# Sum over 1024 columns: 16-row bulk loads, two access patterns and stores instead of three, and the last store ahead of the closing waits

## Chip, cores and metric

One core of a Trainium2 chip. The metric is the time of one execution in device microseconds; medians of several runs. The experiments ran on three different chips, so kernels are compared through the kernel before, which ran in each.

## The reference

```python
batch, seq, dim = 32, 512, 1024          # x is float32, 67.1 MB
def reference(x, divisor):               # divisor = 1024.0
    return (np.sum(x, axis=-1) / divisor).astype(np.float32)
```

16384 rows of 1024 numbers: 128 rows for each of 128 partitions.

## The kernel before

SyncE (SP) issues all loads and stores. Bulk tiles rotate through three buffers; VectorE (DVE) reduces a tile in one instruction, ScalarE (ACT) takes some rows near the end, GpSimd (POOL) scales the result. The last rows come in ever smaller loads, down to two half rows `pa` and `pb`. The rows of a partition lie in two parts of `x`: its first 16 rows (64 KB from one partition to the next, called the pitch) and its other 112 (448 KB). A load or store "lands" when its semaphore, a counter that others wait on, tells that it is complete.

```python
F, L = 16, 16
M = J - F - L                     # J = 128 rows per partition
W = M + L
x_first = bass.AP(tensor=x.tensor, offset=0, ap=[[F * D, P], [D, F], [1, D]])
x_main = bass.AP(tensor=x.tensor, offset=P * F * D, ap=[[W * D, P], [D, M], [1, D]])
x_last = bass.AP(tensor=x.tensor, offset=P * F * D + M * D, ap=[[W * D, P], [D, L], [1, D]])
first = [(2, 0), (14, 0)]                         # (rows, of which on ACT)
main = [(14, 0)] * 5 + [(14, 4), (12, 5)]
last = [(9, 4), (4, 2), (2, 1)]
# ... cut
for loads, src, dst in ((first, x_first, res0), (main, x_main, res)):
    j = 0
    for rows, on_act in loads:
        t = bulk.tile([P, 14, D], F32, name="t")
        load(t[:, :rows, :], src[:, j : j + rows, :])
        d = rows - on_act
        for i in range(d, rows):
            act_sum(dst[:, j + i : j + i + 1], t[:, i, :])
        nc.vector.reduce_sum(out=dst[:, j : j + d], in_=t[:, :d, :], axis=AX)
        j += rows
    nc.gpsimd.tensor_scalar_mul(out=dst, in0=dst, scalar1=scale)
# ... cut: the last loads; stores of res0 and res
dve_mean(pb[:, D - c : D - c + 1], pa, by=1.0)
dve_mean(fin[:, j:], pb)
tc.keep_in_program_order(nc.sync.dma_start(out=o_last, in_=fin))
```

`close_while_storing` rearranges the program's end: SyncE waits for everything but the last store (`drain`), issues that store, takes part in the closing barriers of all five engines, and at last waits until the store has landed. In a closing barrier every engine reports that it is there (SyncE's report is a DRAIN instruction) and goes on when all have reported.

```python
end.instructions = [
    with_sync(drain, on_wait=tuple(needs.values())),
    with_sync(store, on_wait=(done,), on_update=(add,)),   # done: VectorE's last instruction
    *end.instructions[1:-1],                               # the two closing barriers
    with_sync(last, on_update=(sub,)),                     # the store has landed
]
```

Of the kernel before, what the change touches and what calls it, by code (L numbers as in the profile page):

```python
# [9 lines left out]
F32 = mybir.dt.float32  # L10
ADD = mybir.AluOpType.add
COPY = mybir.ActivationFunctionType.Copy
AX = mybir.AxisListType.X
# [23 lines left out]
def with_sync(i, on_wait=None, on_update=None):  # L37
    s = i.sync_info
    return copy.replace(
        i,  # L40
        sync_info=mybir.SyncInfo(
            on_wait=s.on_wait if on_wait is None else on_wait,
            on_update=s.on_update if on_update is None else on_update,
        ),
    )
# [21 lines left out]
def close_while_storing(nc, landed):  # L67


    body, end = nc.main_func.blocks[1], nc.main_func.blocks[-1]  # L70
    store = [i for i in body.instructions if i.engine == SP and type(i).__name__ == "InstDMACopy"][-1]
    (lane,) = store.sync_info.on_update
    drain = end.instructions[0]
    assert drain.engine == SP and type(drain).__name__ == "InstDrain"
    needs = {w.id: w for w in drain.sync_info.on_wait}
    assert needs[lane.id].wait_value > lane.update_value
    needs[lane.id] = dataclasses.replace(
        needs[lane.id], wait_value=needs[lane.id].wait_value - lane.update_value
    )

    (done,) = [w for w in store.sync_info.on_wait if w.ant_name.startswith("DVE_")]
    assert needs[done.id].wait_value == done.wait_value
    del needs[done.id]
    own = dict(sync_type="semaphore", id=landed.num, ant_name=landed.name)
    add = mybir.SyncUpdate(update_mode="sem-add-imm", update_value=16, **own)
    sub = mybir.SyncUpdate(update_mode="sem-sub-imm", update_value=16, **own)
    last = nc.sync.wait_ge(landed, 16).ins
    assert nc.main_func.blocks[-1].instructions[-1].name == last.name
    body.instructions = [i for i in body.instructions if i.name != store.name]
    end.instructions = [  # L90
        with_sync(drain, on_wait=tuple(needs.values())),
        with_sync(store, on_wait=(done,), on_update=(add,)),
        *end.instructions[1:-1],
        with_sync(last, on_update=(sub,)),
    ]


@with_exitstack
def kernel(
    ctx: ExitStack,  # L100
    tc: tile.TileContext,
    x: bass.AP,
    divisor: float,
    out: bass.AP,
):
    nc = tc.nc
    landed = nc.alloc_semaphore("landed")
    nc.at_finalize(start_loads_at_once)
    nc.at_finalize(latest_wait_first)
    nc.at_finalize(lambda nc: close_while_storing(nc, landed))  # L110
    xf = x.flatten_outer_dims()
    N, D = xf.shape
    P = nc.NUM_PARTITIONS
    scale = 1.0 / float(divisor)
    J = N // P
    assert J * P == N


    F, L = 16, 16
    M = J - F - L  # L120
    W = M + L
    x_first = bass.AP(tensor=x.tensor, offset=0, ap=[[F * D, P], [D, F], [1, D]])
    x_main = bass.AP(tensor=x.tensor, offset=P * F * D, ap=[[W * D, P], [D, M], [1, D]])
    x_last = bass.AP(tensor=x.tensor, offset=P * F * D + M * D, ap=[[W * D, P], [D, L], [1, D]])
    o_first = bass.AP(tensor=out.tensor, offset=0, ap=[[F, P], [1, F]])
    o_main = bass.AP(tensor=out.tensor, offset=P * F, ap=[[W, P], [1, M]])
    o_last = bass.AP(tensor=out.tensor, offset=P * F + M, ap=[[W, P], [1, L]])


    first = [(2, 0), (14, 0)]  # L130
    main = [(14, 0)] * 5 + [(14, 4), (12, 5)]
    last = [(9, 4), (4, 2), (2, 1)]
    assert sum(n for n, _ in first) == F
    assert sum(n for n, _ in main) == M and sum(n for n, _ in last) == L - 1

    pad = ctx.enter_context(tc.tile_pool(name="pad", bufs=1))
    pad.tile([P, 224], F32, name="pad")
    bulk = ctx.enter_context(tc.tile_pool(name="bulk", bufs=3))
    one = ctx.enter_context(tc.tile_pool(name="one", bufs=1))
    psum = ctx.enter_context(tc.tile_pool(name="junk", bufs=4, space=bass.MemoryType.PSUM))  # L140


    c = 512
    t4 = one.tile([P, 4, D], F32, name="t4")
    t2 = one.tile([P, 2, D], F32, name="t2")
    pa = one.tile([P, 768], F32, name="pa")[:, :c]
    pb = one.tile([P, D - c + 16], F32, name="pb")[:, : D - c + 2]
    res0 = one.tile([P, F], F32, name="res0")
    res = one.tile([P, M], F32, name="res")
    fin = one.tile([P, L], F32, name="fin")  # L150
    nc.gpsimd.memset(pb[:, D - c :], 0.0)  # L151

    def load(dst, src):
        tc.keep_in_program_order(nc.sync.dma_start(out=dst, in_=src))  # L154

    def act_sum(dst, src, by=1.0):
        junk = psum.tile([P, D], F32, name="junk")
        nc.scalar.activation(junk, src, COPY, scale=by, accum_out=dst)  # L158

    def dve_mean(dst, src, by=scale):  # L160


        h = src.shape[-1] // 2
        nc.vector.tensor_tensor_reduce(  # L164
            out=src[:, :h], in0=src[:, :h], in1=src[:, h:], scale=by, scalar=0.0,
            op0=ADD, op1=ADD, accum_out=dst,
        )

    for loads, src, dst in ((first, x_first, res0), (main, x_main, res)):
        j = 0  # L170
        for rows, on_act in loads:
            t = bulk.tile([P, 14, D], F32, name="t")
            load(t[:, :rows, :], src[:, j : j + rows, :])
            d = rows - on_act
            for i in range(d, rows):
                act_sum(dst[:, j + i : j + i + 1], t[:, i, :])
            nc.vector.reduce_sum(out=dst[:, j : j + d], in_=t[:, :d, :], axis=AX)  # L177
            j += rows
        nc.gpsimd.tensor_scalar_mul(out=dst, in0=dst, scalar1=scale)  # L179
    j = 0  # L180
    for rows, on_act in last:
        t = bulk.tile([P, 14, D], F32, name="t")[:, :rows, :] if rows > 4 else t4 if rows == 4 else t2
        load(t, x_last[:, j : j + rows, :])
        d = rows - on_act
        for i in range(rows):
            if i < d:
                dve_mean(fin[:, j + i : j + i + 1], t[:, i, :])
            else:
                act_sum(fin[:, j + i : j + i + 1], t[:, i, :], by=scale)
        j += rows  # L190
    load(pa, x_last[:, j, :c])
    load(pb[:, : D - c], x_last[:, j, c:])


    tc.keep_in_program_order(nc.sync.dma_start(out=o_first, in_=res0))
    tc.keep_in_program_order(nc.sync.dma_start(out=o_main, in_=res))

    dve_mean(pb[:, D - c : D - c + 1], pa, by=1.0)
    dve_mean(fin[:, j:], pb)
    tc.keep_in_program_order(nc.sync.dma_start(out=o_last, in_=fin))  # L200
# [35 lines left out]
```

## Time and profile before

| | before |
|---|---|
| time, median of the 6 runs beside the changed kernel | 160.75 us (160.63 to 160.82) |
| span of the profiled run | 159.1 us, its time 160.59 us |
| VectorE, ScalarE busy | 117.2 us, 18.5 us |
| DMA queue | 98.2% of 16 engines' span |

The span goes from the first to the last recorded instruction; the time is longer by 1.5 to 1.6 us. The lines of the profile that carry the argument are in the prediction.

### The profile page before, as it was taken

What the parts mean: (1) busy time and instruction counts of PE and PEld (TensorE: products, weight loads), DVE (VectorE), ACT (ScalarE), POOL (GpSimd) and SP (SyncE); (2) the same over time, 40 slices, a digit from 0 to 9 for tenths busy, and PEclk for the clock granted to TensorE, in tenths of its full rate; (3) what the DMA queues carried; (4) which work ended last, traced back from release to release, by engine and by line L of the source; (5) the groups of instructions that cost most, each with busy time, mean ns of one, the idle gap of its engine ahead of it and who ended that gap; (6) DMA issues with size and microseconds to landing.
All of it is one profiled execution on the core that took longest, in us unless ns stands there. A gap on an engine that the chain in (4) does not pass through costs nothing.

```text
span 159.1 us, 147 instructions
## 1 busy us (share of the span) xinstructions
DVE 117.2 (74%) x29; ACT 18.5 (12%) x33; POOL 1.0 (1%) x7
## 2 busy tenths in 40 slices
DVE  0500059995999599977999599959995996395643
ACT  3000000000000000000000000000000900390684
POOL 0000000000000000000000000000000000001000
DMA  8999999979999999789999999699999999999894
GB/s 303 422 461 461 461 461 461 433 317 404 461 461 461 461 461 461 317 375 461 461 461 461 461 461 418 303 433 461 461 461 429 396 396 445 445 445 445 375 406 159
DMA packets 2448, 67.18 MB, mean 422 GB/s; under 512 B 656, under 2 KB 656, under 8 KB 912
## 3 DMA queue, kind: packets, MB, share of 16 engines
q1 hardware_dynamic: 2448, 67.18, 98.2%
HBM read 67.11 MB, written 0.07 MB: 422 GB/s over the span
## 4 chain that ended last, share of the span: by engine, by line
DMA 77%; DVE 21%; SPq 1%; issue 0%; DVEq 0%
DMA t<-in_x_dram 56%; DMA pb<-in_x_dram 21%; DVE res L177 20%; SPq L154 1%; DVE pb L164 0%; DVEq L231 0%
## 5 line engine op out<-in xcount | busy, mean ns | idle before, releaser
L177 DVE TENSOR_REDUCE res<-t 128x14 f32<-128x14336 f32 (+3 forms) x9 | 111.2, 12360 | 34.1 <-DMA t<-in_x_dram 34.1
L158 ACT ACTIVATE junk<-t 128x1024 f32<-128x1024 f32 x16 | 16.2, 1013 | 136.9 <-DMA t<-in_x_dram 136.9
L164 DVE CUSTOM_DVE_ANT_0 t<-t 128x512 f32<-128x512 f32 x8 | 5.1, 690 | 6.1 <-DMA t<-in_x_dram 6.1
L158 ACT ACTIVATION_READ_ACCUMULATOR junk<-t 128x1 f32 x16 | 3.0, 187 | 0.0
L179 POOL TENSOR_SCALAR res<-res 128x16 f32<-128x16 f32 (+1 forms) x2 | 0.7, 352 | 143.3 <-DVE res L177 143.3
L158 ACT ACT_TABLE_LOAD x1 | 1.3, 1283 | 1.7 <-PEq L217 1.7
L164 DVE DVE_READ_ACCUMULATOR2_ANT fin<- 128x1 f32 x9 | 0.8, 83 | 0.0
L164 DVE CUSTOM_DVE_ANT_0 pb<-pb 128x257 f32<-128x257 f32 x1 | 0.4, 428 | 0.2 <-DMA pb<-in_x_dram 0.2
L164 DVE CUSTOM_DVE_ANT_0 pa<-pa 128x256 f32<-128x256 f32 x1 | 0.4, 426 | 0.0
L151 POOL MEMSET pb<- 128x2 f32 x1 | 0.1, 99 | 1.3 <-POOLq L217 1.3
L217 POOL MEMSET const-bfloat16-1.0<- 128x1 bf16 x1 | 0.1, 102 | 0.0
L217 POOL MEMSET const-uint8-127<- 128x1 uint8 x1 | 0.1, 101 | 0.0
L217 POOL MEMSET const-float32-0.0<- 128x1 f32 x1 | 0.1, 98 | 0.2 <-issue 0.2
L217 POOL MEMSET const-float32-1.0<- 128x1 f32 x1 | 0.1, 98 | 0.0
L164 DVE DVE_READ_ACCUMULATOR2_ANT pb<- 128x1 f32 x1 | 0.1, 84 | 0.0
## 6 DMA issues: line engine op xcount, KB each, us to landing
t<-in_x_dram SPq DMA_DIRECT2D x7, 7168.0 KB, 35.6
t<-in_x_dram SPq DMA_DIRECT2D x1, 6144.0 KB, 33.3
t<-in_x_dram SPq DMA_DIRECT2D x1, 4608.0 KB, 27.2
t<-in_x_dram SPq DMA_DIRECT2D x2, 1024.0 KB, 19.2
t<-in_x_dram SPq DMA_DIRECT2D x1, 2048.0 KB, 31.7
pa<-in_x_dram SPq DMA_DIRECT2D x1, 256.0 KB, 33.9
pb<-in_x_dram SPq DMA_DIRECT2D x1, 256.0 KB, 33.9
out_dram<-res SPq DMA_DIRECT2D x1, 48.0 KB, 11.6
```

The source lines that it names most:

```text
L151: nc.gpsimd.memset(pb[:, D - c :], 0.0)
L154: tc.keep_in_program_order(nc.sync.dma_start(out=dst, in_=src))
L158: nc.scalar.activation(junk, src, COPY, scale=by, accum_out=dst)
L164: nc.vector.tensor_tensor_reduce(out=src[:, :h], in0=src[:, :h], in1=src[:, h:], scale=by, scalar=0.0, op0=ADD, op1=ADD, accum_out=dst,)
L177: nc.vector.reduce_sum(out=dst[:, j : j + d], in_=t[:, :d, :], axis=AX)
L179: nc.gpsimd.tensor_scalar_mul(out=dst, in0=dst, scalar1=scale)
L217: nc = _bacc.Bacc("TRN2", target_bir_lowering=False, num_devices=1)
```

## The change

Its intent: fewer and larger loads, one store fewer, and a last store that need not queue behind the closing waits. Core of the diff (the tile shapes follow; a tile for 4 rows goes, `pa` shrinks):

```diff
     end.instructions = [
+        with_sync(store, on_wait=store.sync_info.on_wait, on_update=(add,)),
         with_sync(drain, on_wait=tuple(needs.values())),
-        with_sync(store, on_wait=(done,), on_update=(add,)),
         *end.instructions[1:-1],
@@
-    F, L = 16, 16
-    M = J - F - L
-    W = M + L
-    x_first = ...  x_main = ...  x_last = ...  o_first = ...  (cut)
-    first = [(2, 0), (14, 0)]
-    main = [(14, 0)] * 5 + [(14, 4), (12, 5)]
+    L = 16
+    M = J - L
+    x_main = bass.AP(tensor=x.tensor, offset=0, ap=[[M * D, P], [D, M], [1, D]])
+    x_last = bass.AP(tensor=x.tensor, offset=P * M * D, ap=[[L * D, P], [D, L], [1, D]])
+    main = [(2, 0), (14, 0)] + [(16, 0)] * 4 + [(16, 4), (16, 7)]
@@
-            t = bulk.tile([P, 14, D], F32, name="t")
+        t = bulk.tile([P, 16, D], F32, name="t")
@@
-    tc.keep_in_program_order(nc.sync.dma_start(out=o_first, in_=res0))
     tc.keep_in_program_order(nc.sync.dma_start(out=o_main, in_=res))
```

## The prediction

> **What bounds the kernel now.** I read the page from the top: busy shares, the transfer rows, the chain that ended last, then the timeline of VectorE (DVE) and of the end. VectorE is busy 117.2 of 159.1 us, ScalarE (ACT) 18.5 us, so neither fills the span. The DMA queue does:
>
> ```profile
> DMA packets 2448, 67.18 MB, mean 422 GB/s; under 512 B 656, under 2 KB 656, under 8 KB 912
> q1 hardware_dynamic: 2448, 67.18, 98.2%
> ```
>
> 98.2% of the 16 DMA engines' time is in packets, and 67.11 of the 67.18 MB are the input, read once. The chain that ended last seems to say something else, 77% DMA and 20% of VectorE's reduce. That share is how the view follows a load back to the wait of its issue, a buffer freed by a reduce. It doesn't mean that the queue stood still, which the spacing of the reduces shows:
>
> ```profile
> 21.60 15.09 DVE L177 TENSOR_REDUCE res<-t 128x14 f32<-128x14336 f32 x1 [14.60 <-DMA t<-in_x_dram]
> ...
> 38.51 15.09 DVE L177 TENSOR_REDUCE res<-t 128x14 f32<-128x14336 f32 x1 [1.83 <-DMA t<-in_x_dram]
> 55.46 15.09 DVE L177 TENSOR_REDUCE res<-t 128x14 f32<-128x14336 f32 x1 [1.86 <-DMA t<-in_x_dram]
> 72.39 15.09 DVE L177 TENSOR_REDUCE res<-t 128x14 f32<-128x14336 f32 x1 [1.84 <-DMA t<-in_x_dram]
> 89.28 15.09 DVE L177 TENSOR_REDUCE res<-t 128x14 f32<-128x14336 f32 x1 [1.80 <-DMA t<-in_x_dram]
> 106.19 15.09 DVE L177 TENSOR_REDUCE res<-t 128x14 f32<-128x14336 f32 x1 [1.83 <-DMA t<-in_x_dram]
> ```
>
> Each reduce starts when its load lands, each after about 1.8 us of idling, and the landings are (106.19 - 21.60) / 5 = 16.92 us apart. In the trace's packet records a 14-row load is 8 packets of 57344 bytes per DMA engine at 2.116 us (median), and 8 x 2.116 = 16.93 us. So there is no gap between one load and the next: the engines run packet after packet. The rate row has dips (317 GB/s beside 461), but the load that landed across one (38.51 to 55.46, 16.95 us) took no longer than the one without (55.46 to 72.39, 16.93 us); I take the dips for the booking of packets and not for pauses.
>
> The end is a series of its own:
>
> ```profile
> 122.67 0.47 SPq L154 DMA_DIRECT2D pa<-in_x_dram  x1
> ...
> 123.19 0.44 SPq L154 DMA_DIRECT2D pb<-in_x_dram  x1
> 123.68 0.44 SPq L195 DMA_DIRECT2D out_dram<-res  x1
> ...
> 145.89 0.34 SPq L196 DMA_DIRECT2D out_dram<-res  x1
> ...
> 157.15 0.43 DVE L164 CUSTOM_DVE_ANT_0 pb<-pb 128x257 f32<-128x257 f32 x1 [0.16 <-DMA pb<-in_x_dram]
> 157.50 0.08 DVE L164 DVE_READ_ACCUMULATOR2_ANT fin<- 128x1 f32 x1
> 157.62 0.33 SPq L200 DMA_DIRECT2D out_dram<-fin  x1
> ```
>
> ```profile
> pb<-in_x_dram SPq DMA_DIRECT2D x1, 256.0 KB, 33.9
> out_dram<-res SPq DMA_DIRECT2D x1, 48.0 KB, 11.6
> out_dram<-res SPq DMA_DIRECT2D x1, 8.0 KB, 33.6
> out_dram<-fin SPq DMA_DIRECT2D x1, 8.0 KB, 1.4
> ```
>
> The last column is us from issue to landing. The last half row pb lands at 123.19 + 33.9 = 157.1; VectorE ends at 157.50 + 0.08 = 157.58; the last store is issued at 157.62 and lands 1.4 us later, at 159.02; the span ends at 159.05. So the span is about 4.7 us to the first landing (start, and 2 rows), 152.4 us of packets, and 1.9 us of end. The timed run is 160.74 us, 1.6 us above the span.
>
> **What the Trainium skill says.** "DMA: Bandwidth & Descriptors", section "Where 436 GB/s comes from", gives 435.2 GB/s as the ceiling of a core's DMA. The trace agrees: from the 8192-byte packet (0.309 us) to the 57344-byte one (2.116 us) the slope is 36.76 ns per 1000 bytes, or 27.2 GB/s per engine and 435 GB/s for 16. What is left over is 0.309 - 0.301 = 0.008 us per packet. The same page, "Queues, rings and completion order", has each engine consume descriptors in ring order. The trace agrees: the 8 KB store was issued at 123.68, 34 us ahead of the end, and landed at 157.3, behind pb. The same page, "Latency and other measured facts" (row "HBM row pitch at large powers of two"), tells of copies slowed by pitches from 512 KiB up; it lists neither 64 nor 448 KB. Here the first 16 rows have 64 KB between partitions and the rest 448 KB: the 14-row load of the first part took 21.60 - 4.72 = 16.88 us, the 448 KB ones 16.92. Neither is slowed.
>
> **The change part by part.** The bytes are the same. Five things move.
>
> (1) Loads: 14 become 13, so 104 packets per engine in place of 112, and one completion write (0.009 us in the records) fewer: 8 x 0.008 + 0.009 = 0.07 us less. All of it lies on the path, as the packets are the bound. A 65536-byte packet should take 0.008 + 2.409 = 2.417 us, and a 16-row load 8 x 2.417 + 0.009 = 19.35 us.
>
> (2) VectorE: 2 rows took 2.285 us and 14 rows 15.085, so 1.067 us a row and 0.15 fixed: 16 rows are 17.22 us, 2.1 us under their load's 19.35. Three buffers are kept. A buffer is free 17.2 us after its landing; by then one load has 2.1 us to go and another is queued whole, so the next is issued some 21 us ahead of its turn (1.8 + 16.9 = 18.7 us before). The two mixed loads: 12 rows on VectorE, about 12.95 us, and 9 rows, 9.75 us, with ScalarE's 7 rows at 1.04 us, 7.3 us, beside them. The last of these lands at about 137.6 and is done at 147.4, a good 1 us before the 9-row load at 148.5. The 4-row load now takes a bulk buffer and waits for the reduce that ends at about 118.3 + 12.95 = 131.3; the queue holds work until 148.5. Nothing waits.
>
> (3) Stores: the 8 KB store goes, and the other grows from 48 to 56 KB. Both lay behind pb in the ring and before the last store (landed at 157.29 and 157.46). Their 16 packets per engine were under the time of VectorE's last two halves. Worth 0 on the path.
>
> (4) Pitch: the first 16 rows go from 64 to 448 KB, the last 16 from 448 to 64 KB. By the two durations above, 0, with perhaps 0.1 us either way at the first packets, some of which took up to 1.06 us in place of 0.309.
>
> (5) The last store ahead of the closing waits. SyncE's own waits in the view of waits, as they are now:
>
> ```profile
> SPq L231 <- DMA t<-in_x_dram: 9.7, 1, 9.7
> SPq L231 <- DMA pa<-in_x_dram: 0.6, 1, 0.6
> SPq L231 <- DMA pb<-in_x_dram: 0.6, 1, 0.6
> ```
>
> They run beside the last loads. The records of SyncE's semaphore instructions have the last of them at 157.476 and its drain at 157.541, so SyncE stood at the store by about 157.6, as VectorE ended (157.58); it started at 157.615. A store usually starts 0.02 to 0.03 us after what it waits for, so at most 0.01 us is won. But the five waits and the drain now stand behind the store. Between store and final wait are two rounds of the closing barrier, from 157.998 to 158.768, under the store's flight, which ends at 159.02: 0.25 us of slack. A satisfied wait costs about 0.065 us (157.476 to 157.541), so six cost about 0.39 us (an estimate; at 0.05 each, 0.30). That is 0.05 to 0.14 us more than the slack: the barrier, and no longer the store, would end the program.
>
> Sum: -0.07 - 0.01 + 0.09 (the middle of the last) = +0.01 us, so 160.75 us.
>
> **The rivals.** *Fixed cost per transfer*: if each load paid a start-up on the path, say 1.4 us as the last store alone, one fewer would give 159.3. Against it: landings 16.92 us apart are packets alone. *VectorE becomes the bound*, or buffers come free too late: its digits stand at 9 in most slices, but 17.22 / 19.35 is 0.89, as 15.09 / 16.93 is now. If the queue did run dry once per buffer round, six bulk loads with 0.5 to 1 us each would make 164 to 167. *Pitch or packet size matters after all*: 64 KB packets may be cut in two, which costs 6 x 8 x 0.008 = 0.4 us (161.1); if the last 16 rows at 64 KB ran a fifth slower, 19 us become 23, and the time 164.6. Against it stands the first load of before. *The end*: if the store was held up by the closing waits in most runs (they pass just 0.04 us before VectorE is done in this one), moving it wins about 0.1 us, and with (1) the time is 160.55; if the waits behind it cost more than thought, 160.95.
>
> **Range and chances.** Terms (1) and (5) move the time by hundredths to one or two tenths; the three runs of before span 0.09 us, and the profiled run, at 160.59, adds 0.15. So 160.75, with 160.45 to 161.1 for 8 in 10. A gain of 2% needs 157.5 us, but the bytes alone take 4194304 x 36.76e-6 = 154.2 us per engine, with about 2.3 us before, 1.9 after and 1.6 outside the span: 160.0. Faster by over 2% has 0.5%; slower by over 2% (pitch, cut packets, a dry queue) 1.5%; within it 98%.
>
> **What the profile after would show.** Reduces of 16 rows at 17.2 us, starting 19.35 us apart with 2.1 us of idling; 65536-byte packets of 2.417 us, 104 load packets per engine; pb landing at about 157.05; VectorE done 0.45 us later; the last store some 0.03 us after that, landing in 1.4 us; SyncE's waits between the store and the barrier, with the barrier's end at or behind the landing. It would be wrong if the landings of bulk loads are not 19.35 us apart, if VectorE's idle before a reduce is near 0, if the last four loads take more than 10.8, 4.9, 2.5 and 1.2 us (the last the two halves together), or if the span's end moves against pb's landing by over 0.2 us.

## More of the kernel before

All runs here are at a granted clock of 1.00.

One view of before is added here because it becomes the key: SyncE's semaphore and drain instructions of the closing block, and its last wait (times: ns shortest/median/longest, then the us at which the first and the last of them start).

```profile
L231 SPq EVENT_SEMAPHORE  x7: 17/27/28, 155.9 to 158.8; - x7
L231 SPq DRAIN  x3: 7/7/129, 157.5 to 158.4; - x3
L87 SPq EVENT_SEMAPHORE  x1: 17/17/17, 159.0 to 159.0; - x1
```

Five of the seven are closing waits, begun at 155.9 us while the last loads still run; the other two belong to the barriers, and the last, at 158.8, is SyncE leaving the second one. L87 is the wait for the landing.

## The result and the profile after

161.02 us (160.90 to 161.36, 6 runs) against 160.75 us (160.63 to 160.82, 6 runs): ratio 1.0019, interval [1.0006, 1.0032]. A ratio is the mean time of one kernel's fast runs over the mean of the other's in the same rounds, so not quite the ratio of these medians. The change is small, but it is a loss.

The transfer rows of the changed kernel's page, with the rate of each fortieth of the span:

```profile
GB/s 245 479 461 461 461 527 263 526 494 296 527 378 411 526 263 527 526 263 526 527 263 526 526 263 527 526 263 526 461 329 526 329 461 526 296 444 444 383 406 150
DMA packets 2161, 67.18 MB, mean 422 GB/s; under 512 B 497, under 2 KB 497, under 8 KB 753
q1 hardware_dynamic: 2160, 67.18, 98.1%
```

The queue is as full as before, with 288 packets fewer (2160 for 2448: a load and a store, each of 128 and 16 completion writes). The rate now swings between 263 and 527 GB/s. The view books a packet whole in the slice in which it starts; with the packets' bytes spread over their durations, the records give 425 to 434 GB/s in every 4 us from 4 to 156, before and after. So these are no pauses. Landings are even too, as the timeline of VectorE's bulk reduces shows:

```profile
41.04 17.22 DVE L170 TENSOR_REDUCE res<-t 128x16 f32<-128x16384 f32 x1 [4.25 <-DMA t<-in_x_dram]
60.42 17.22 DVE L170 TENSOR_REDUCE res<-t 128x16 f32<-128x16384 f32 x1 [2.17 <-DMA t<-in_x_dram]
79.74 17.22 DVE L170 TENSOR_REDUCE res<-t 128x16 f32<-128x16384 f32 x1 [2.10 <-DMA t<-in_x_dram]
99.05 17.22 DVE L170 TENSOR_REDUCE res<-t 128x16 f32<-128x16384 f32 x1 [2.09 <-DMA t<-in_x_dram]
```

(99.05 - 41.04) / 3 = 19.34 us for a load, 2.1 us of idling before a reduce: both as predicted. A packet of 65536 bytes takes 2.418 us (median). The stream of loads is what the prediction said it would be.

The end, in the timeline:

```profile
157.38 0.43 DVE L158 CUSTOM_DVE_ANT_0 pb<-pb 128x257 f32<-128x257 f32 x1 [0.20 <-DMA pb<-in_x_dram]
157.74 0.08 DVE L158 DVE_READ_ACCUMULATOR2_ANT fin<- 128x1 f32 x1
157.85 0.34 SPq L192 DMA_DIRECT2D out_dram<-fin  x1
```

The store starts 0.03 us after VectorE's end (157.82), as before. It lands 1.41 us later, as before. Up to there nothing is lost but 0.23 us in the loads of this one profile, which the experiments show to be scatter. What moved is behind the store. SyncE's closing instructions now:

```profile
L223 SPq EVENT_SEMAPHORE  x7: 17/28/28, 158.2 to 159.2; - x7
L223 SPq DRAIN  x3: 7/7/7, 158.5 to 158.8; - x3
L88 SPq EVENT_SEMAPHORE  x1: 17/17/17, 159.3 to 159.3; - x1
```

All seven stand behind the store: none starts before 158.2. In the records the five waits, long satisfied, start 0.053 to 0.065 us apart, from 158.243 to 158.484, then the drain at 158.549. SyncE reports to the first barrier at 158.607, 0.76 us after the store's start; before, it did so at 157.998, 0.38 us after. (That this report lasted 0.129 us before, and 0.007 now, gives 0.12 us back.) SyncE leaves the second barrier 1.406 us after the store's start instead of 1.153: 0.25 us later.

My prediction had seen this, and had set 0.25 us of slack against it, until the landing. The profiles contradict the slack:

| profiled run | SyncE leaves second barrier | SyncE's last wait ends | time | time less barrier | time less last wait |
|---|---|---|---|---|---|
| before | 158.77 | 159.05 | 160.59 | 1.82 | 1.54 |
| after | 159.25 | 159.33 | 161.08 | 1.83 | 1.75 |

The time is a constant after the barrier, not after the landing. (SyncE stands here for all engines: they leave the second barrier within 0.07 us of one another in every profile, so the record can't say which of them counts.) All runs say so through their spans, which end with the last wait: time less span is 1.50 to 1.60 us in every run of before that was timed beside an experiment, and 1.75 to 1.80 in the six of the changed kernel.

### The profile page after: what moved, and what is told of

It is laid out like the page before. It is cut to its first block, busy times and chain, and to the rows that moved or that the text cites. A ratio compares the mean times of both kernels' runs of the same rounds, so it can differ in the third digit from the quotient of the medians.

```text
span 159.3 us, 148 instructions
## 1 busy us (share of the span) xinstructions
DVE 115.0 (72%) x28; ACT 20.5 (13%) x37; POOL 0.8 (0%) x6
## 3 DMA queue, kind: packets, MB, share of 16 engines
q1 hardware_dynamic: 2160, 67.18, 98.1%
## 4 chain that ended last, share of the span: by engine, by line
DMA 66%; DVE 30%; another core or an unknown queue 1%; SPq 1%; issue 0%; DVEq 0%
DMA t<-in_x_dram 51%; DVE res L170 30%; DMA pb<-in_x_dram 15%; SPq L148 1%; DVE pb L158 0%; DVEq L223 0%
## 5 line engine op out<-in xcount | busy, mean ns | idle before, releaser
L170 DVE TENSOR_REDUCE res<-t 128x16 f32<-128x16384 f32 (+4 forms) x8 | 109.0, 13620 | 38.6 <-DMA t<-in_x_dram 38.6
L152 ACT ACTIVATE junk<-t 128x1024 f32<-128x1024 f32 x18 | 18.2, 1012 | 134.9 <-DMA t<-in_x_dram 134.9
L172 POOL TENSOR_SCALAR res<-res 128x112 f32<-128x112 f32 x1 | 0.5, 492 | 145.8 <-DVE res L170 145.8
```

Of the source, the lines that this page charges most:

```text
L152: nc.scalar.activation(junk, src, COPY, scale=by, accum_out=dst)
L170: nc.vector.reduce_sum(out=res[:, j : j + d], in_=t[:, :d, :], axis=AX)
L172: nc.gpsimd.tensor_scalar_mul(out=res, in0=res, scalar1=scale)
```

## The experiments

The theory at this point (A in the first four, D later): the order at the end costs time, because the barrier ends the program. A counted only how far the barrier overshoots the landing; D takes the landing to be off the path. The rivals: the layout (B), the 64 KB packets (C), the landing (E). Twelve kernels were run, 5 rounds each; all were correct.

### e1: the changed kernel with the old closing order

```diff
-        with_sync(store, on_wait=store.sync_info.on_wait, on_update=(add,)),
         with_sync(drain, on_wait=tuple(needs.values())),
+        with_sync(store, on_wait=(done,), on_update=(add,)),
```

> The changed kernel with the closing waits ahead of the last store again. Theory A (the order at the end costs, the barrier now ends after the store has landed): the final wait passes about 0.02 us after the landing, as before (0.055 us after it in the changed kernel), and the time falls by 0.04 to 0.1 us, to 160.92-160.98. Theory B (the layout costs: first landing 0.11 us later at 448 KB, and the 9-row load 0.16 us longer at 64 KB): both stay, the time stays at 160.95-161.05, with first landing near 4.81 and the 9-row load near 11.0 us. Theory C (bulk packets of 64 KB cost): as B, with the bulk loads to blame.

160.69 us (160.65 to 160.81); ratio to before 0.9996 [0.9983, 1.0009]. More came back than theory A allowed, which counted only the overshoot past the landing. Time less barrier is 1.83 us again, time less last wait 1.54. With the end undone, no loss that this interval resolves is left in the loads, the packets and the stores.

### e2: the kernel before with the new closing order

```diff
+        with_sync(store, on_wait=store.sync_info.on_wait, on_update=(add,)),
         with_sync(drain, on_wait=tuple(needs.values())),
-        with_sync(store, on_wait=(done,), on_update=(add,)),
```

> The kernel before with the last store ahead of the closing waits, nothing else. Theory A: 160.80-160.85, the SyncE waits stand between store and barrier and the barrier ends 0.05 us or more after the landing. If the store was really held up before: 160.65. Theories B and C: 160.75, first landing 4.70, 9-row load 10.84.

160.85 us (160.82 to 160.93); ratio 1.0006 [0.9994, 1.0018]. By the clock alone this is unclear: the interval holds both 0 and 0.25 us. The profile is clearer: the barrier ends 1.39 us after the store's start (1.15 before), and time less pb's landing is 160.85 - 157.15 = 3.70 us, against 160.59 - 157.13 = 3.46 before. All its five runs have 1.71 to 1.75 us between time and span.

### e3: the kernel before with 16-row loads

```diff
-    main = [(14, 0)] * 5 + [(14, 4), (12, 5)]
+    main = [(16, 0)] * 4 + [(16, 4), (16, 7)]
```

(the tile shapes that follow are cut; pitches, three stores and closing order stay)

> The kernel before with 16-row bulk loads, one load fewer, its pitches, three stores and closing order kept. By my sum of packets: 0.07 us less, 160.68. Theory C (64 KB packets or their buffers cost): 160.85 or more. Theory B: first landing 4.70 and the 9-row load 10.84 us, as the pitches are those of before.

160.79 us (160.71 to 161.37); ratio 1.0006 [0.9993, 1.0018]. Neither the gain of 0.07 us nor a loss is resolved. Its first landing came at 4.83 us, though the first part had its old pitch: theory B's 4.70 was a miss, and the first landing turned out to scatter (4.53 to 4.96 us over all profiles).

### e4: the new layout with 14-row loads and the old closing order

```diff
-    main = [(2, 0), (14, 0)] + [(16, 0)] * 4 + [(16, 4), (16, 7)]
+    main = [(2, 0)] + [(14, 0)] * 6 + [(14, 4), (12, 5)]
```

(against the changed kernel; the tile shapes and the closing order of before are cut)

> The changed kernel's layout and its two stores, with the loads (14 rows), the tile for 4 rows and the closing order of the kernel before. Theory B: first landing 4.81 and the 9-row load 11.0 us, time 160.95-161.05. Theories A and C: 160.75, first landing 4.70, 9-row load 10.84.

160.75 us (160.68 to 161.10); ratio 1.0003 [0.9991, 1.0014]. The median fits A and C. The profiled run was the slowest of the five: its 9-row load took 11.17 us, its last 14-row load 17.15, where 10.85 and 16.95 are usual. That kept theory B alive.

### e5: SyncE reports to the barrier ahead of the store

On the kernel before; VectorE's last instruction is waited for in the report, the store follows it (the comments stand for code that is cut).

```diff
     end.instructions = [
         with_sync(drain, on_wait=tuple(needs.values())),
-        with_sync(store, on_wait=(done,), on_update=(add,)),
-        *end.instructions[1:-1],
+        # SyncE's report to the first barrier, now waiting for `done` too
+        # the store, without a wait
+        # the rest of the two barriers
```

> The kernel before, but SyncE reports to the first closing barrier ahead of the last store (it waits for VectorE in that report, so the store still comes after). In the six profiles so far the time is the end of the second closing barrier plus 1.82-1.83 us, whether or not the store has landed by then. Theory D (the barrier sets the time, SyncE's own wait for the landing lies beside it): the barrier ends about 0.3 us earlier, near 158.45, and the time is 160.3-160.4. Theory E (the landing sets the time, at 1.54 us behind SyncE's last instruction): the store starts 0.06 us later, so 160.8.

160.60 us (160.56 to 160.93); ratio 0.9992 [0.9974, 1.0010]. Both theories missed. In the profile, taken from the slowest of the six runs, the barrier ended at 158.84, and 1.83 us on top would be 160.67, but the time was 160.93. It is 1.33 us behind the end of SyncE's last wait (159.60): the landing took over, at a smaller constant than E had.

### e6: six more waits behind the store

On the kernel before: six further SyncE instructions between store and barrier, each waiting for what has long come (the program has twelve waits, which the trace shows in pairs).

> The kernel before with six more satisfied wait instructions on SyncE between the last store and the closing barrier. Theory D: each costs its 0.063 us in full, 0.38 us in all, 161.1; time minus span rises from 1.55 to about 1.75. Slack theory of my prediction (0.25 us are free until the landing): 0.13 to 0.17 us, 160.9, with time minus span still 1.55.

160.95 us (160.86 to 161.18); ratio 1.0011 [0.9994, 1.0028]. The six, as a view of their line shows them (ns, then first and last start):

```profile
L87 SPq EVENT_SEMAPHORE  x6: 27/28/28, 158.1 to 158.4; - x6
```

An instruction takes 0.028 us, but the next starts 0.059 to 0.064 us after it. The barrier ends 1.40 us after the store's start, 0.25 us later than before, and the time of the profiled run is 1.83 us after that. The 0.38 us of theory D was a miss in size: it overlooked that SyncE's report to the barrier, 0.129 us long when it directly follows the store, is over in 0.007 when it comes later. The slack theory missed in kind: time less span is 1.72 to 1.78 us.

### e7: the store after SyncE's report to the second barrier

On the kernel before: the store moved further back than in e5.

> The kernel before with the last store issued after SyncE's report to the second closing barrier, so that it starts 0.3-0.4 us later and the barrier ends 0.4-0.5 us earlier. Shows what follows SyncE's last wait: if the landing takes over, the time is landing plus some constant up to 1.54 us, at most 161.0; if the barrier still sets the time, 160.1-160.2.

160.82 us (160.77 to 161.28); ratio 1.0006 [0.9985, 1.0026]. The barrier ended at 158.45, earliest of all, and the store started 0.45 us after VectorE. Time less last wait is 1.33 us, as in e5; time less barrier 2.37. So in these kernels two paths end the program, and the later one sets the time.

### e8: the changed kernel with e5's end

> The changed kernel's layout, loads and two stores, with the closing order of e5. If the layout and loads are worth under 0.1 us, it lies within 0.1 us of e5, and by theory D 0.5-0.6 us under the changed kernel: 160.3-160.45. By theory E: 160.75.

160.69 us (160.59 to 161.03); ratio 0.9997 [0.9979, 1.0016], and 0.09 us above e5. Profile: last wait at 159.34, time 160.67, again 1.33 us apart.

### e9 and e10: an early report and a store that starts at once

e5 lost some time ahead of the store, because SyncE waited for VectorE in the report and only then went on. Here VectorE's last instruction raises a semaphore of its own (`ready`), which the barrier's clearing does not touch; SyncE reports to the barrier without waiting for VectorE (which reports for itself), and the store waits for `ready`. e9 is the kernel before with this end, e10 the changed kernel with it (comments stand for cut code).

```diff
+    # VectorE's last instruction counts up `ready` in place of its usual semaphore
     end.instructions = [
         with_sync(drain, on_wait=tuple(needs.values())),
-        with_sync(store, on_wait=(done,), on_update=(add,)),
-        *end.instructions[1:-1],
+        # SyncE's report to the first barrier
+        # the store, waiting for `ready`
+        # the rest of the two barriers
+        # wait for `ready` again, to set it back to 0
```

> The kernel before with SyncE's report to the first closing barrier ahead of the last store, and a semaphore of its own between VectorE's last instruction and the store, so that the store starts as early as before. In ten profiles the time is the later of two: end of the second barrier + 1.83 us, and end of SyncE's last wait + 1.33 us. Before, the first leads by 0.21 us. Here the store starts 0.03 us after VectorE, the barrier ends about 0.7 us behind that start, so the landing leads: VectorE's end + 0.03 + 1.43 + 1.33, 0.2 us under before: 160.5, time minus span 1.33. If a third path ends the program, it stays at 160.7.

> The changed kernel's layout, loads and stores with the closing of e9: 0.42-0.45 us under the changed kernel in the same rounds, 160.5-160.6, and within 0.15 us of e9, as layout and loads have shown nothing clear of noise.

e9: 160.63 us (160.51 to 160.69), ratio to before 0.9989 [0.9977, 1.0001]. e10: 160.62 us (160.49 to 160.77), ratio to before 0.9991 [0.9979, 1.0003]; its mean over that of the changed kernel in the same rounds is 160.63 / 161.06 = 0.997, with ranges that don't overlap; the two differ in the end alone. The landing leads in both, as foretold, but e9 gained half of the 0.2 us. The timeline of e9's end shows the rest:

```profile
157.70 0.08 DVE L178 DVE_READ_ACCUMULATOR2_ANT fin<- 128x1 f32 x1
157.87 0.33 SPq L214 DMA_DIRECT2D out_dram<-fin  x1
```

VectorE is done at 157.78, and the store starts 0.09 us later instead of 0.03 (0.11 in e10). The records have the big store landed at 157.653; the last of the closing waits follows at 157.670, the drain at 157.735, the report at 157.793, the store at 157.874. In e3, without a report between, the store came 0.06 us after the drain; here that would be 157.80 (an estimate), no later than VectorE's end and the usual 0.03 us. So it is the report, which this end puts ahead of the store, that takes back the missing 0.06 to 0.08 us; in e10 the same sum holds (drain 157.703, report 157.761, store 157.842, VectorE's end 157.734).

The closing waits themselves clearly held the last store up in one profile: in e3 the second store landed at 157.606, two waits and the drain still had to pass, and the last store started 0.07 us after VectorE instead of 0.03. That hold-up is what the change set out to remove; in the profile of before it was not there.

### e11: the changed kernel again

> The changed kernel itself beside the others: 161.0, time minus span 1.75-1.8, barrier end + 1.83. If the 64 KB pitch slows the last 16 rows, the 9-row load takes over 10.9 us again (10.85-10.87 in all profiles at 448 KB, and 11.00, 10.88, 11.17, 10.87 at 64 KB).

161.05 us (160.89 to 161.22); ratio to before 1.0018 [1.0005, 1.0030]. Time less barrier 1.83, time less span 1.72 to 1.80. Its 9-row load at 64 KB took 10.87 us, and that of e9, at 448 KB, took 10.99. With that theory B falls: slow packets come now and then in either layout (e5's profile has four loads between 16.98 and 17.12 us in place of 16.9, at the old pitches).

### e12: one part, 512 KB from partition to partition

e1 with all 128 rows of a partition together. (The output patterns follow; the edit is against the changed kernel, the old closing order is cut.) The row of the skill that the expectation names is "HBM row pitch at large powers of two" in "DMA: Bandwidth & Descriptors", section "Latency and other measured facts". It is of copies between HBM tensors, so what it makes of loads into SBUF, 165 us, is an estimate.

```diff
-    x_main = bass.AP(tensor=x.tensor, offset=0, ap=[[M * D, P], [D, M], [1, D]])
-    x_last = bass.AP(tensor=x.tensor, offset=P * M * D, ap=[[L * D, P], [D, L], [1, D]])
+    x_main = bass.AP(tensor=x.tensor, offset=0, ap=[[J * D, P], [D, M], [1, D]])
+    x_last = bass.AP(tensor=x.tensor, offset=M * D, ap=[[J * D, P], [D, L], [1, D]])
```

> e1 (the changed kernel with the old closing order) with one part only: every partition's 128 rows lie together, 512 KB apart. Pitch has shown no effect between 64 and 448 KB beyond 0.1-0.3 us in one load. If 512 KB is slowed by the 3% that the skill's row has (207 against 214 GB/s), the bulk loads take 19.9 us in place of 19.33 and the time is 165; if not, 160.7.

161.19 us (161.15 to 161.32); ratio 1.0027 [1.0015, 1.0039]. Pitch does matter, at 512 KB, but neither as little nor as much as either guess. In the timeline of its bulk reduces:

```profile
41.16 17.22 DVE L170 TENSOR_REDUCE res<-t 128x16 f32<-128x16384 f32 x1 [4.53 <-DMA t<-in_x_dram]
60.54 17.22 DVE L170 TENSOR_REDUCE res<-t 128x16 f32<-128x16384 f32 x1 [2.16 <-DMA t<-in_x_dram]
80.25 17.22 DVE L170 TENSOR_REDUCE res<-t 128x16 f32<-128x16384 f32 x1 [2.48 <-DMA t<-in_x_dram]
99.53 17.22 DVE L170 TENSOR_REDUCE res<-t 128x16 f32<-128x16384 f32 x1 [2.06 <-DMA t<-in_x_dram]
```

Two loads took 0.3 to 0.4 us too long (the third landing comes 80.25 - 60.54 = 19.71 us after the second, and the first one here came 0.3 late too); the others 19.3 to 19.4. What in those two loads is slow stays open. The run shows that keeping the rows in two parts is worth about half a microsecond (ratio to before 0.9996 for e1, 1.0027 here), and both the kernel before and the changed one have that.

### The two ends of all fourteen profiles

The later of "barrier left + 1.83" and "last wait ended + 1.33" against the time of the same run:

| | barrier + 1.83 | last wait + 1.33 | time |
|---|---|---|---|
| before | **160.60** | 160.38 | 160.59 |
| after | **161.08** | 160.66 | 161.08 |
| e1 old close | **160.65** | 160.44 | 160.65 |
| e2 new close | **160.85** | 160.43 | 160.85 |
| e3 16 rows | **160.79** | 160.57 | 160.79 |
| e4 layout | **161.10** | 160.88 | 161.10 |
| e5 report first | 160.67 | **160.93** | 160.93 |
| e6 more waits | **160.95** | 160.53 | 160.95 |
| e7 store late | 160.28 | **160.82** | 160.82 |
| e8 after, report first | 160.40 | **160.67** | 160.67 |
| e9 own semaphore | 160.38 | **160.65** | 160.63 |
| e10 after, own semaphore | 160.36 | **160.62** | 160.60 |
| e11 after again | **161.10** | 160.68 | 161.10 |
| e12 one part | **161.15** | 160.94 | 161.15 |

The constants come from the first six rows (1.83) and from e5, e7 and e8 (1.33). The largest miss is 0.02 us. What fills these 1.83 and 1.33 us is in no trace. The Trainium skill, "Runtime: NRT & Kernel Launch", section "The ~15µs preamble/postamble breakdown", lists instructions that the runtime puts behind a kernel: a `sync_barrier` and a `sema_reset` of about 1.5 us each, then a `sync_barrier` with `dma_rearm` of about 2 us. Their sum, about 5 us by the page's figures, is not the 1.83 or 1.33 us here, and no run here shows these instructions. Why there are two starting points, one at the barrier and one at SyncE's last wait, stays open.

## Why the prediction held, and where it did not

Predicted 160.75 us, range 160.45 to 161.1; measured 161.02. The sum was off by 0.27 us, and one term of it, (5), holds 0.17 of that. That the time lies inside the range is partly luck: without the 0.12 us that the shorter report gave back, which the prediction didn't see, it would have been about 161.14.

**What bounds the kernel**: right. Landings of 16-row loads lie 19.34 us apart (19.35 predicted), VectorE takes 17.22 us and idles 2.1, packets take 2.418 us (2.417). The dips of the rate row are booking, as was said, but the check of it proved nothing: they move with the width of the slices (63.6 to 71.6 us in the row, 70 to 80 us in windows of 2 us), and by the row the load that was taken for the one without a dip holds one. And "1.6 us above the span" set one run's time against another's span; the profiled run is at 1.54.

**(1), 0.07 us fewer packets**: not resolved. From the first landing to pb's takes a median of 152.44 us in the six profiles with 16-row loads (e12 left out) and 152.47 in the seven with 14-row loads, with single profiles from 152.3 to 153.0. A gain of that size may be there; e3's clock doesn't show it.

**(2) and (3), buffers and stores**: right. Nothing waited: e1, which has the new loads, layout and stores with the old end, stands at 0.9996 of before.

**(4), pitch worth 0**: right for 64 against 448 KB within the scatter (e4: 1.0003 [0.9991, 1.0014]); the first landing and the 9-row load, which looked guilty in the first pair of profiles, scatter in every kernel.

**(5), the end**: this is the step that failed. The predicted cost of the six satisfied instructions, about 0.39 us, was right (0.76 - 0.38 = 0.38 us from the store's start to the report). What failed was "0.25 us of slack" behind it: I took the landing of the last store for the end of the program, since the last recorded instruction waits for it. The landing was 0.22 us off the path before (160.60 against 160.38 in the table), and the barrier was on it. So the barrier's delay counted in full. The term was booked at +0.09 - 0.01; it measures +0.25, the 0.38 us of the waits less 0.12 that the shorter report gave back: from the store's start to the end of the barrier it is 1.15 us in before and 1.16 in e1, against 1.39 to 1.41 in the changed kernel, e2, e6 and e11. By the clock e2 and e6 alone show 0.10 and 0.18 us more than before, with intervals that hold both 0 and 0.25. -0.07 - 0.01 + 0.25 would have made 160.92, 0.1 us off.

**The rival of the end** was named ("if the waits behind it cost more than thought, 160.95") and is what came, though for another reason: the waits cost what was thought, their shelter did not exist.

## What to carry to other kernels

When time less span differs between two kernels, something that the trace doesn't record sits on the path: look for a recorded event that stands at a constant distance from the time over many runs, rather than taking the last instruction for the end. Behind the last store, each satisfied wait or drain ahead of the closing barrier cost about 0.06 us here; ahead of it, the waits were free as long as all of them had passed before the last result (e3 is where they had not). With the queue at 98%, 16-row loads for 14-row ones and one store fewer were worth nothing that 5 rounds could resolve.

The version to take further is e9 or e10 (160.63 and 160.62 us, 0.1 us under before, with intervals that still hold 1, so not shown, and 0.4 us under the changed kernel): an end that lets the barrier run beside the store. Putting the closing waits behind the barriers, beside the store's flight, might win another 0.06 to 0.1 us (an estimate from the gaps in e9 and e10); it was not tried, as GpSimd clears semaphores between the two barriers, by my reading of the program these among them.

## What the Trainium skill lacked or had wrong

- "Runtime: NRT & Kernel Launch" lists what follows a kernel, but not from where it counts: here the time was the later of barrier left + 1.83 us and last wait + 1.33 us, in 14 profiles, within 0.02 us.
- No page has the cost of a satisfied wait on SyncE: 0.017 to 0.028 us in the record, 0.053 to 0.065 us from one to the next.
- "DMA: Bandwidth & Descriptors", row "HBM row pitch at large powers of two", is of copies between HBM tensors (512 KiB at 207 GB/s, against 214 at full rate); it has no loads into SBUF. Here loads at 512 KB made the whole kernel 0.3% slower than e1 (ratios to before 1.0027 and 0.9996), in two loads that took 0.3 to 0.4 us longer; 64 and 448 KB, which it doesn't list, show no difference.
- The same page tells the fixed cost of a packet for small packets only. On the way from HBM to SBUF it was 0.008 us each from 8192 bytes to 65536 (0.309, 2.116 and 2.418 us), at 27.2 GB/s for one engine.
